# Storing the gate sigmoids beside the attention from GpSimd's queue, not ScalarE's

## The chip, the core and the metric

The kernel runs on one core of one Trainium2 chip. The core has five engines that matter here, each with its own instruction queue that is worked off in order: TensorE (PE in the profile, with PEld for its weight loads), VectorE (DVE), ScalarE (ACT), GpSimd (POOL) and SyncE (SP). ACT, POOL and SP can also issue DMA transfers; an issue stands in the queue of the engine that issues it. The metric is the device time of one execution in microseconds, lower is better, as the median of several runs.

## The reference

One layer of a streaming encoder trunk, in float32, for two request groups: 512 prompt tokens, and 8 streams of 16 tokens with cached keys and values. All 640 rows are worked together. Cut to what matters:

```python
parts = jnp.split(rms_norm(x, g_pre) @ w_in, points, axis=-1)
sb_q, sb_k, sb_v, sb_g, bd_q, bd_k, bd_v, bd_g, mm_q, mm_g, mg_sb, mg_bd, mg_mm = parts
o_sb = stick_breaking(...)      # 6 heads, strictly causal
o_bd = band_attention(...)      # 6 heads, softmax over a band, with a bias
o_mm = memory_attention(...)    # 4 heads into 256 memory tokens
merged = (jax.nn.sigmoid(mg_sb) * branch(o_sb, sb_g, w_up_sb)
          + jax.nn.sigmoid(mg_bd) * branch(o_bd, bd_g, w_up_band)
          + jax.nn.sigmoid(mg_mm) * branch(o_mm, mm_g, w_up_mem))
return x + rms_norm(merged @ w_out, g_post)
```

The three merge gates `mg_sb`, `mg_bd` and `mg_mm` are 2048 columns each, so 48 blocks of 128 columns. The change touches how the sigmoids of half of them reach memory.

## The kernel before, in words

Every float32 matrix product is made of three passes over operands that are split into a high and a low part (`split`, L118 to L120: ScalarE rounds the high part, VectorE subtracts it). Weights come by SP's queue into `wr` (L146) and are split into `wh` and `wl` (L119, L120), four buffers each.

The work runs in stages. First the memory projection and the normalisation of x. Then the projection of x, most of it in pairs of column blocks (`block_pair`, products at L760), up to about 1075 us of the profiled span. Next comes the attention, 16 heads in the order of `ORDER`, with the last 24 of the 48 gate blocks (`BESIDE`) spread among its steps as filler for TensorE. After it come the up-projections of the three branches, the merge and the output projection.

A gate block beside the attention is `gate_steps` (L694): 96 matmuls into a PSUM tile `acc` (L191, in four steps of 24), one ScalarE sigmoid from `acc` into `sig` (L698), and a store of `sig` to a DRAM tile `sig_d[i]` (L692) of 320 KB. `sig` has three buffers (pool `stg`). The same `put_sig` also stores the gates of the stage before (`put_gate`, L817). The stored gates are read back in the up-projections (L905), branch after branch, so the last 24 are read last.

`fill` (L920) pulls the next step of the filler; the attention's own matmuls stand between those steps, and `issue_after` chains the steps on TensorE in this order. The order of the other engines' queues, and the waits between them, are laid down when the kernel is compiled, from a simulated timeline (L1052).

A stick-breaking head takes, for each of four blocks of 128 queries: scores on TensorE into `s` (L176 to L178), two sigmoids on ScalarE into `b` and `e` (L430, L431), two masks on GpSimd (L433), a running product over `e` (L485) and a product with `b` (L487) on VectorE, and, about one filler step later on TensorE, the transposes of `b` into `tp` (L451). From `tp` ScalarE and VectorE make the split weights `wth` and `wtl`, and TensorE multiplies them with the values into `o`. The cached keys come in `kc` (L535, SP's queue), are transposed by VectorE into `kt` (L545) and multiplied at L549. GpSimd has little else in this stage: stores of new values (L643, L646) and of each head's result `osg_d` (L617), clears of `wth` and `wtl` (L445), and a mask product (L567).

Of the kernel before, what the change touches and what calls it, by code (L numbers as in the profile page):

```python
# [48 lines left out]
def stream_step_kernel(  # L49
# [8 lines left out]
    PE, ACT, DVE, POOL, SP = nc.tensor, nc.scalar, nc.vector, nc.gpsimd, nc.sync  # L58
# [42 lines left out]
    sig_d = [dpool.tile([P, NT], F32, name=f"sig_d{i}") for i in range(3 * KB)]  # L101
# [16 lines left out]
    def split(hi, lo, src):  # L118
        ACT.copy(hi, src)  # L119
        DVE.tensor_tensor(lo, src, hi.bitcast(F32), op=ALU.subtract)  # L120
# [79 lines left out]
    def x_proj_steps(col, acc):  # L200

        nonlocal last_mm, back
        steps, back = proj_steps(w_in, col, KB, x_src, acc, 8, back), False
        for _ in range(KB // 4):
            with tc.issue_after(last_mm or last_on(PE)):
                next(steps)
            last_mm = last_on(PE)
            yield
# [5 lines left out]
    def new_acc():  # L214
        return ps_acc.tile([P, 2, 512], F32, tag="acc", name="acc")

    def halves(t):
        return t.rearrange("p (s n) -> p s n", s=2)
# [469 lines left out]
    def operand(n, pool):  # L688
        return tuple(pool.tile([P, KH, HF], F32R, name=f"t{c}{n}") for c in "hl")

    def put_sig(i, sig):
        ACT.dma_start(sig_d[i], sig)  # L692

    def gate_steps(i):  # L694
        acc = new_acc()
        yield from x_proj_steps(C_GATE + i * P, acc)
        sig = stg.tile([P, NT], F32, tag="sig", name="sig")
        ACT.activation(halves(sig), acc[:, :, :HF], AF.Sigmoid)  # L698
        put_sig(i, sig)

    t2, t1 = operand(2, tpool), operand(1, tpool)
    tpool2 = gs.enter_context(tc.tile_pool(name="tpool2", bufs=1, reuse_waits="tile"))
# [23 lines left out]
    for i in range(FIRST):  # L726
        for _ in gate_steps(i):
            pass
        third.append(sums(2 * i))
# [80 lines left out]
    def put_gate(i):  # L810
        def put(n, t, q):
            if q is None:
                ACT.activation(t, t, AF.Sigmoid)
            else:
                ACT.activation(t[:, HF:], t[:, HF:], AF.Sigmoid)
                ACT.activation(t[:, :HF], q, AF.Sigmoid)
            put_sig(i + n, t)  # L817
        return put
# [46 lines left out]

    def fill_steps(done):
        for i in gates[-BESIDE:]:
            yield from gate_steps(i)

        xs.close()  # L870
        pm = br.enter_context(tc.tile_pool(name="mraw", bufs=1, side="right", reuse_waits="tile"))
        merged = pm.tile([P, KB, NT], F32, name="merged")
        po = br.enter_context(tc.tile_pool(name="osgp", bufs=6, side="right", reuse_waits="tile"))

        def load_o(i):
            r = po.tile([P, NT], F32, tag="sig", name="or", bufs=4)
            SP.dma_start(r, osg_d[i])
            hh = po.tile([P, NT], F32R, tag="oh", name="oh")
            ll = po.tile([P, NT], F32R, tag="ol", name="ol")
            split(hh, ll, r)  # L880
            return hh, ll

        for n, (w_up, nh, i0, g0) in enumerate(branches):
            while not done.issuperset(range(i0, i0 + nh)):
                yield
            parts = [load_o(i0 + h) for h in range(nh)]

            def o_src(k):
                return [[t[:, j * HF:(j + 1) * HF] for j in range(2)] for t in parts[k]]

            for j in range(KB):
                yield from up_steps(w_up, nh, o_src, j, n, merged[:, j], g0, po)
        up_done.append(merged)

    def up_steps(w_up, nh, src, j, n, m, g0, po):
        nonlocal last_mm
        acc = new_acc()
        steps = proj_steps(w_up[0], j * P, nh, src, acc)
        for _ in range((nh + 3) // 4):
            with tc.issue_after(last_mm):  # L900
                next(steps)
            last_mm = last_on(PE)
            yield
        sig = po.tile([P, NT], F32, tag="sig", name="sig", bufs=4)
        SP.dma_start(sig, sig_d[g0 + j])  # L905
        if n == 0:
            DVE.tensor_tensor(halves(m), acc[:, :, :HF], halves(sig), op=ALU.mult)
        else:
            DVE.tensor_tensor(halves(sig), acc[:, :, :HF], halves(sig), op=ALU.mult)
            POOL.tensor_tensor(m, m, sig, op=ALU.add)  # L910

    up_done = []
    with tc.tile_pool(name="att", bufs=1, reuse_waits="tile") as pa:
        qm, wTm = zero_padded(4)


        rest, done = iter(()), set()
        filler = fill_steps(done)

        def fill(n=1):  # L920
# [135 lines left out]
```

## Time and profile before

| what | us |
|---|---|
| median of 3 runs | 2049.0 |
| lowest and highest | 2047.3, 2050.6 |
| span of the profiled execution | 2044.4 |
| attention with the 24 gate blocks, in the span | about 1076 to 1545 |

Of the profiled execution the page gives the span alone, from its first to its last instruction. The clock that TensorE was granted has a mean of 0.997 over the span. In the views, a timeline row gives the start and the length in microseconds, the engine, the line of the kernel, the operation with output and input, and in square brackets how long the engine stood idle before it and what ended that. A row of waits gives the waiting engine and line, what it waited for, the total, the number and the longest. ACTq, SPq and POOLq are the instruction queues, where DMA issues stand.

### The profile page before, as it was taken

What the parts mean: (1) busy time and instruction counts of PE and PEld (TensorE: products, weight loads), DVE (VectorE), ACT (ScalarE), POOL (GpSimd) and SP (SyncE); (2) the same over time, 40 slices, a digit from 0 to 9 for tenths busy, and PEclk for the clock granted to TensorE, in tenths of its full rate; (3) what the DMA queues carried; (4) which work ended last, traced back from release to release, by engine and by line L of the source; (5) the groups of instructions that cost most, each with busy time, mean ns of one, the idle gap of its engine ahead of it and who ended that gap; (6) DMA issues with size and microseconds to landing.
All of it is one profiled execution on the core that took longest, in us unless ns stands there. A gap on an engine that the chain in (4) does not pass through costs nothing.

```text
span 2044.4 us, 35948 instructions
## 1 busy us (share of the span) xinstructions
PE 2014.2 (99%) x13829; PEld 1908.3 (93%) x13829; DVE 1178.5 (58%) x1830; ACT 839.1 (41%) x1577; POOL 705.8 (35%) x685
## 2 busy tenths in 40 slices
PE   8999999999999999999999999999999999999998
PEld 5999999999999999999998899999998899998886
DVE  6875577655676655555555555555556675442234
ACT  6544444444444444444443444444444332322221
POOL 1145566665666665644431011011010024330000
PEclk9999999999999999999999999999999999999999
DMA  7656676665686564663338777677679876532225
GB/s 269 218 140 150 169 207 142 168 168 149 161 205 154 137 156 130 150 150 111 118 106 280 224 221 219 214 225 225 211 214 283 255 234 178 144 123 83 73 93 216
DMA packets 548185, 361.38 MB, mean 177 GB/s; under 512 B 249169, under 2 KB 493409, under 8 KB 546477
## 3 DMA queue, kind: packets, MB, share of 16 engines
q1 hardware_dynamic: 528414, 305.80, 53.5%
q0 software_dynamic: 12688, 37.57, 5.5%
q10 hardware_dynamic: 6912, 15.73, 2.1%
q8 instruction: 108, 1.77, 0.4%
q14 instruction: 63, 0.52, 0.1%
HBM read 303.17 MB, written 90.77 MB: 193 GB/s over the span
## 4 chain that ended last, share of the span: by engine, by line
PE 91%; DMA 3%; DVE 2%; issue 1%; ACT 1%; POOL 1%; SPq 0%; ACTq 0%; DVEq 0%; POOLq 0%
PE q L760 44%; PE acc L191 27%; PE ya L176 4%; PE ya L178 4%; PE ya L177 4%; PE s L549 2%; PE o L608 1%; DMA or<-osg_d 1%; DVE wl L120 1%; PE tp L451 1%; PE acc L178 1%; PE acc L176 1%; PE acc L177 1%; PE o L177 1%; PE o L178 0%
## 5 line engine op out<-in xcount | busy, mean ns | idle before, releaser
L120 DVE TENSOR_TENSOR wl<-wr,wh 128x512 fp32r<-128x512 f32 (+1 forms) x516 | 411.7, 803 | 301.0 <-ACT wh L119 298.0
L119 ACT CAST wh<-wr 128x512 fp32r<-128x512 f32 (+1 forms) x516 | 311.7, 608 | 564.3 <-PE q L760 214.8
L120 DVE TENSOR_TENSOR wl<-ws,wh 128x512 fp32r<-128x512 f32 x304 | 285.1, 943 | 235.8 <-ACT wh L119 230.0
L760 PE MATMUL q<-xh,wl 128*128 128x320 f32 x1216 | 375.8, 309 | 0.3 <-DVE wl L120 0.3
L760 PE MATMUL q<-xh,wh 128*128 128x320 f32 x1216 | 375.7, 309 | 0.0
L760 PE MATMUL q<-xl,wh 128*128 128x320 f32 x1216 | 375.6, 309 | 0.0
L119 ACT CAST wh<-ws 128x512 fp32r<-128x512 f32 x304 | 188.1, 621 | 291.4 <-PE q L760 236.6
L760 PE MATMUL q<-th,wh 128*128 128x320 f32 x912 | 282.2, 309 | 2.0 <-ACT sig L777 2.0
L760 PE MATMUL q<-th,wl 128*128 128x320 f32 x912 | 281.9, 309 | 0.0
L760 PE MATMUL q<-tl,wh 128*128 128x320 f32 x912 | 281.8, 309 | 0.0
L760 PEld LDWEIGHTS q<-xh,wl 128*128 128x128 f32 x1216 | 228.7, 188 | 0.5 <-DVE wl L120 0.5
L760 PEld LDWEIGHTS q<-xl,wh 128*128 128x128 f32 x1216 | 228.6, 188 | 0.0
L760 PEld LDWEIGHTS q<-xh,wh 128*128 128x128 f32 x1216 | 228.5, 188 | 0.0
L191 PE MATMUL acc<-xh,wh 128*128 128x320 f32 x896 | 210.8, 313 | 0.0
L191 PE MATMUL acc<-xl,wh 128*128 128x320 f32 x896 | 209.5, 311 | 0.0
L191 PE MATMUL acc<-xh,wl 128*128 128x320 f32 x896 | 207.4, 310 | 0.0
L753 POOL TENSOR_TENSOR ws<-wr 128x512 f32<-128x512 f32 x114 | 169.1, 1496 | 81.2 <-DVE wl L120 68.5
L760 PEld LDWEIGHTS q<-th,wh 128*128 128x128 f32 x912 | 171.2, 188 | 2.7 <-ACT sig L777 2.5
L760 PEld LDWEIGHTS q<-th,wl 128*128 128x128 f32 x912 | 171.2, 188 | 0.2 <-DVE wl L120 0.2
L760 PEld LDWEIGHTS q<-tl,wh 128*128 128x128 f32 x912 | 171.2, 188 | 0.0
L191 PEld LDWEIGHTS acc<-xh,wh 128*128 128x128 f32 x896 | 150.1, 188 | 18.9 <-issue 18.4
L191 PEld LDWEIGHTS acc<-xl,wh 128*128 128x128 f32 x896 | 151.2, 188 | 0.6 <-issue 0.4
(228 smaller groups left out, 3353.1 us busy)
## 6 DMA issues: line engine op xcount, KB each, us to landing
wr<-in_w_in_dram SPq DMA_DIRECT2D x208, 512.0 KB, 4.9
kc<-keys_d SPq DMA_DIRECT2D x48, 512.0 KB, 5.8
wr<-in_w_out_dram SPq DMA_DIRECT2D x32, 512.0 KB, 3.7
sig_d<-sig ACTq DMA_DIRECT2D x48, 320.0 KB, 5.1
sig<-sig_d SPq DMA_DIRECT2D x48, 320.0 KB, 3.6
keys_d<-in_cache_sb_k_dram SPq DMA_DIRECT2D x96, 128.0 KB, 4.7
keys_d<-in_cache_band_k_dram SPq DMA_DIRECT2D x96, 128.0 KB, 4.5
vc<-in_cache_sb_v_dram SPq DMA_DIRECT2D x48, 256.0 KB, 5.6
```

Source lines behind the costliest of these rows:

```text
L119: ACT.copy(hi, src)
L120: DVE.tensor_tensor(lo, src, hi.bitcast(F32), op=ALU.subtract)
L176: PE.matmul(out, ah, bh, start=start, stop=False)
L177: PE.matmul(out, ah, bl, start=False, stop=False)
L178: PE.matmul(out, al, bh, start=False, stop=stop)
L191: PE.matmul(acc[:, s, :HF], a[:, k], b[s], start=first and f, stop=last and l)
L451: PE.transpose(tp[:, kb * P:(kb + 1) * P], b[:, kb * P:(kb + 1) * P], ident)
L549: return PE.matmul(s[32 * j:32 * j + 32, :nc_], qm[:, j, par * 32:par * 32 + 32], kts[j], start=par == 0, stop=par == 1, tile_position=(0, ...
L608: PE.matmul(o[32 * j:32 * j + 32, :P], l, r, start=i == 0, stop=i == len(steps) - 1, tile_position=(0, 32 * j))
L753: eng.tensor_tensor(o, a[c], b[c], op=op)
L760: PE.matmul(bank_, a[:, k], b[:, k], start=first and k == 0 and n == 0, stop=k == KH - 1 and n == 2, skip_group_check=not first)
```

## The change

`put_sig` and `gate_steps` take a queue, ScalarE's by default, and `fill_steps` passes GpSimd's. So the 24 stores of the gate blocks beside the attention are issued by POOL; the four gate blocks at the start and those of `put_gate` stay on ACT.

```diff
-    def put_sig(i, sig):
-        ACT.dma_start(sig_d[i], sig)
-
-    def gate_steps(i):
+    def put_sig(i, sig, queue=ACT):
+        queue.dma_start(sig_d[i], sig)
+
+    def gate_steps(i, queue=ACT):
...
-        put_sig(i, sig)
+        put_sig(i, sig, queue)
...
         for i in gates[-BESIDE:]:
-            yield from gate_steps(i)
+            yield from gate_steps(i, POOL)
```

## The prediction, made before the changed kernel was run

> **What bounds the kernel now.** I read the page's first part, then the busy times of the stretch 1076 to 1545 us, the only one the change touches.
>
> ```profile
> span 2044.4 us, 35948 instructions
> PE 2014.2 (99%) x13829; PEld 1908.3 (93%) x13829; DVE 1178.5 (58%) x1830; ACT 839.1 (41%) x1577; POOL 705.8 (35%) x685
> ...
> 1076.00:1545.00 469.00, 462.24 (x3733) 428.39 (x3731) 258.99 (x529) 209.44 (x416) 47.38 (x130) 0.99 0.74 229
> ```
>
> The columns of the last row are PE, PEld, DVE, ACT and POOL. PE is busy for 462.2 of 469.0 us, ACT for 45% and POOL for 10%. Relieving ACT or loading POOL therefore counts only where PE waits for one of them. So the second view is PE's waits in that stretch, which are all of these:
>
> ```profile
> PE tp L451 <- DVE b L487: 4.3, 1, 4.3
> PE o L176 <- ACT wth L119: 2.3, 1, 2.3
> PE tp L451 <- DVE b L497: 0.2, 1, 0.2
> ```
>
> One wait of 4.3 us is most of it. The third view is ACT's timeline before it, the fourth the chain of waits through it.
>
> ```profile
> 1090.26 0.70 ACT L698 ACTIVATE sig<-acc 128x640 f32<-128x640 f32 x1
> 1101.03 0.39 ACTq L692 DMA_DIRECT2D sig_d<-sig  x1
> 1101.47 0.58 ACT L119 CAST wth<-tp 128x512 fp32r<-128x512 f32 x1 [10.51 <-DMA kc<-keys_d]
> ```
> ```profile
> 1093.66 7.30 DMA kc<-keys_d
> ...
> 1100.98 0.02 ACTq L692
> ...
> 1102.45 0.39 ACT e L431
> ...
> 1102.90 0.30 POOL e L433
> ...
> 1104.68 0.56 DVE b L487
> ...
> 1105.38 0.88 PE tp L451 x3
> ...
> 1106.89 3.88 PE acc L191 x21
> ...
> 1110.89 0.44 PE acc L191 x3
> 1111.33 0.12 PE s L176
> ```
>
> The first gate's sigmoid ends at 1090.96, but its store is issued only at 1101.03, 10.07 us later, right when a load of cached keys, issued by SP, lands. `sig` and `kc` share no data, so I take it that the store waits on a completion count that the two transfers share. ACT's queue is in order: behind the store stand the cast of `wth`, then the sigmoids L430 and L431, and from them the chain runs over POOL's mask, DVE's product and PE's transposes. I conclude this from the ACTq step in the chain: the cast itself needs `tp`, which PE had made by about 1094.4 (below), and no `kc`.
>
> The Trainium skill, "DMA: Bandwidth & Descriptors", section "Why a DMA increments its semaphore by 16 and not by 1", says that two transfers in flight on one semaphore can be mistaken for each other and asks for one semaphore per slot in flight. A store that waits for the earlier holder of its semaphore is what that would lead to; the trace shows the wait, not the semaphore's number.
>
> **What the change removes.** The store leaves ACT's queue, so the cast could run when `tp` is ready.
>
> ```profile
> 1093.81 0.60 PE L451 MATMUL tp<-ident,b 128*128 128x128 f32 x4
> ...
> 1094.77 0.31 PE L191 MATMUL acc<-xh,wh 128*128 128x320 f32 x1
> ...
> 1100.79 0.31 PE L191 MATMUL acc<-xh,wh 128*128 128x320 f32 x1
> ```
>
> The scores s are done by about 1095, so what took 4.28 us from L430's start at 1101.95 to the transposes at 1105.38 (3.4 us) would end near 1098.5, before PE gets there at 1100.94 (1100.79 plus a matmul's pace). The stall of 1105.38 − 1100.94 = **4.44 us** goes.
>
> ```profile
> 687.53 387.68 PE q L760 x2640
> ...
> 1106.00:1110.00 4.00, 4.00 (x22) 4.00 (x21) 3.96 (x8) 1.76 (x4) 0.96 (x3) 0.69 1.11 343
> ```
>
> The pace undisturbed is 387.68 / 2640 = 0.147 us a matmul. After the stall the granted clock is 0.69 in 1106 to 1110 us. From 1105.38 to 1111.33 PE took 5.95 us for 3 transposes, 3 scores, 24 gate matmuls and one L176. At full clock that is at most 0.96 us for the transposes and scores (the four and three of 1093.81 to 1094.77), 24 × 0.147 = 3.53, and 0.12: 4.61. So another **1.34 us** goes. If the clock dips all the same, this term is nothing.
>
> What is late next at that place? The second pair of keys, and the weights of the next gate steps:
>
> ```profile
> 1096.10 1.43 SPq L535 DMA_DIRECT2D kc<-keys_d  x1
> ...
> 1098.66 2.16 SPq L146 DMA_DIRECT2D wr<-in_w_in_dram  x1
> ...
> DMA to landing us min/median/max: 7.3/7.5/7.8
> ...
> 1102.70 1.15 ACT L119 CAST wh<-wr 128x512 fp32r<-128x512 f32 x2
> ...
> 1111.61 1.05 PE L549 MATMUL s<-kt,qm 128*32 128x512 f32 x4
> ```
>
> The keys land by 1096.10 + 7.8 = 1103.9, and the matmuls on them would come at 1111.6 − 5.8 = 1105.8; two transposes of DVE lie between (the row at L545 below: 0.65 us each). The weight casts ran at 1102.70 back to back, so their data was there by then; one is used at once, the other a step later. I take nothing for this; at worst 1 us comes back.
>
> ```profile
> 1105.15 1.30 DVE L545 STREAM_TRANSPOSE kt<-kc 128x512 f32<-128x512 f32 x2
> L692 ACTq DMA_DIRECT2D sig_d<-sig x25: 326/327/393, 1076.1 to 1540.5; - x25
> L837 POOL DMA_DIRECT2D raw_d<-sig x28: 540/558/591, 158.4 to 780.4; - x28
> ```
>
> The other 23 stores free ACT for 23 × 0.327 = 7.5 us in all, of which PE gets nothing: it waits for ACT only once more (2.3 us). That wait is set by a table load and the last sigmoid, not by a store:
>
> ```profile
> 1538.46 1.28 ACT L698 ACT_TABLE_LOAD   x1
> 1539.75 0.70 ACT L698 ACTIVATE sig<-acc 128x640 f32<-128x640 f32 x1
> ```
>
> **What it adds.** 24 stores on POOL, of the size of the 28 at L837: 24 × 0.558 = 13.4 us, which raises POOL from 47.4 to 60.8 us of 469, or 13%. POOL's work in this stage that PE hangs on is the pair of masks. Each store needs the sigmoid done on ACT, a wait that is new on POOL; behind it queue the next masks, clears or head stores. In the order of time the closest POOL instruction behind a sigmoid's end is this one:
>
> ```profile
> 1331.71 0.70 ACT L698 ACTIVATE sig<-acc 128x640 f32<-128x640 f32 x1
> ...
> 1333.29 0.54 POOL L617 DMA_DIRECT2D osg_d<-sg  x1 [0.98 <-DVE sg L616]
> ```
>
> 0.88 us lie between, more than 0.558. So, if POOL's queue keeps the order of time, no mask is delayed: nothing. The upper bound is in the rivals. A store may itself stand behind POOL's waits, of which the longest in the stretch is 23.7 us:
>
> ```profile
> POOL wtl L445 <- PE o L177: 147.9, 15, 23.7
> ```
>
> That delays only the release of `sig`, which has three buffers for a gate every (1539.75 − 1090.26) / 23 = 19.5 us, and the reads come later, the 24 last gates at the end. Nothing again. The `put_gate` stores, and everything ahead of 1076 us, stay.
>
> A rule of the Trainium skill speaks against the change. "SBUF — State Buffer", section "SBUF: two separate sides", says that a DMA issued from GpSimd has its descriptors written by GpSimd's cores, which a VectorE instruction that holds the shared port pair locks out, and "A bandwidth-pool intuition that's wrong (but worth ruling out)" gives 3100 ns for a DMA that takes 620 alone; by it the sum would get up to 24 × 2.5 = 60 us of POOL time, an estimate from that page. The L837 rows disagree: 28 stores, beside a VectorE that is busy 63% of that stage, all took 0.540 to 0.591 us.
>
> ```profile
> 150.00:850.00 700.00, 698.49 (x4760) 697.77 (x4759) 444.18 (x507) 293.55 (x527) 453.56 (x385) 1.00 0.64 159
> ```
>
> **The sum.** 4.44 + 1.34 = 5.8 us, bounds 3.4 (the clock dip stays, 1 us comes back) and 8.1 (the wait of 2.3 us goes too). The profiled execution's span would be 2038.6. The span lies 4.6 us under the median of the runs, which I take as what lies around it: 2049.0 − 5.8 = **2043.2 us**. A measurement can tell about 0.2% here, 4.1 us.
>
> **The rivals.** (1) *The wait moves along with the store.* If the store on POOL also waits for the keys, the mask behind it (1102.90 in the chain) is as late as now and the same stall stands: 2049. Against it: the stores at L837 wait for SP's loads hardly at all.
>
> ```profile
> POOL raw_d L837 <- DMA keys_d<-in_cache_band_k_dram: 0.9, 3, 0.3
> ```
>
> (2) *The orders are laid down anew.* The queues follow a simulated timeline (L1052), and a store off ACT changes it. One more stall of the 2.3 us kind with its clock dip costs about 3.6 us, so a single one leaves 2046.8, and two make 2050.4: within 0.2%. Against it: the stalls are very few, since almost everything has a filler step of slack.
>
> (3) *Slower: POOL stands ahead of its masks.* If a store stands before a mask whose input is ready, the mask waits for the sigmoid. Its price: table load, sigmoid, store.
>
> ```profile
> L698 ACT ACT_TABLE_LOAD  x12: 1283/1283/1283, 1140.9 to 1538.5; - x12
> ```
>
> 1.28 + 0.70 + 0.56 = 2.54 us each where PE has no slack, in up to 12 gates (those with a table load). From the third one the gain is gone (5.8 / 2.54 = 2.3), from the fourth it is slower by over 0.2%; six give 2049.0 − 5.8 + 15.2 = 2058.4, all twelve 2073.7. For it: the transposes can follow the masks closely, 2.5 us at 1102.90 to 1105.38. Against it: the order of time above, and a step of 24 × 0.147 = 3.5 us of filler before most transposes.
>
> (4) *VectorE holds the stores up.* If a store can't be written while a VectorE instruction runs, it waits for the end of it, at most about as long as this one:
>
> ```profile
> 1103.22 0.96 DVE L485 TENSOR_TENSOR_SCAN e<-e 128x384 f32<-128x384 f32 x1 [0.44 <-POOL e L433]
> ```
>
> If all 24 did, and PE felt each, that is 23 us on the sum, 2066; the L837 rows leave it hardly a chance. This is the mechanism of the Trainium skill's rule above ("SBUF — State Buffer").
>
> That the change doesn't do what it says isn't possible: `fill_steps` passes POOL to all 24.
>
> **Chances.** Forecast as it stands, 2041.5 to 2044.9: 0.50. More than that, if the other small waits go too: 0.05. Rival 1: 0.08. Rival 2 and a part-gain within 0.2%: 0.20. Rival 3, with a bad new order among its causes: 0.16. Rival 4: 0.01. So faster 0.55, same 0.28, slower 0.17. The range runs from 2040.5 to 2055: about 0.03 lies under it and 0.11 above.
>
> **What would show it.** Right: in the changed trace no ACT idle of 10 us near 1091, L692 on POOL with about 0.56 us each, no PE wait at L451 near 1101, the granted clock back at 1.00 there, the attention ending near 1539 instead of 1545, and the same distance from there to the end. Wrong: a POOL wait on `kc` or on `sig` of several us with a PE wait on L451 behind it; or PE waits at new places; or the 5.8 us given back at the change to the up-projections, where PE now waits for `or`.

## The result, and the profile after

The changed kernel takes 2045.3 us (median of 20 runs, 2040.5 to 2047.9) against 2048.95 for the kernel before (20 runs, 2044.1 to 2054.5). The ratio is 0.998 with a 95% interval of 0.9973 to 0.9987, so 2.7 to 5.5 us less, 4.1 by the ratio. The forecast was 5.8 us less.

The first part of the page of the changed kernel, and PE's waits in its attention stage:

```profile
span 2044.8 us, 36000 instructions
PE 2016.7 (99%) x13829; PEld 1910.4 (93%) x13829; DVE 1178.1 (58%) x1830; ACT 837.9 (41%) x1577; POOL 719.3 (35%) x709
```

```profile
PE o L176 <- ACT wth L119: 2.3, 1, 2.3
PE acc L191 <- DVE ol L120: 0.6, 1, 0.6
PE s L549 <- DVE kt L545: 0.5, 1, 0.5
```

The wait of 4.3 us at L451 is gone, the one of 2.3 us stands as before, and two short ones are new. Yet this span is no shorter than the 2044.4 us of before: single executions of one kernel differ by several microseconds, as the medians' ranges show, so two spans alone decide nothing here. Note also that PE is busy 2.5 us longer (2014.2 before) with the same 13829 matmuls. Two things that lengthen it are found below.

ACT's timeline of the changed kernel at the place of the old stall, and POOL's:

```profile
1091.92 0.70 ACT L698 ACTIVATE sig<-acc 128x640 f32<-128x640 f32 x1
1096.10 0.59 ACT L119 CAST wth<-tp 128x512 fp32r<-128x512 f32 x1 [3.48 <-PE tp L451]
...
1110.18 0.62 ACT L119 CAST wh<-wr 128x512 fp32r<-128x512 f32 x1 [6.00 <-DMA wr<-in_w_in_dram]
```

```profile
1093.96 0.54 POOL L692 DMA_DIRECT2D sig_d<-sig  x1
1097.19 0.29 POOL L433 TENSOR_SCALAR_AFFINE_SELECT b<-b 128x128 f32<-128x128 f32 x1 [2.69 <-ACT b L430]
```

The cast of `wth` now waits 3.48 us for `tp`, which it needs, where it stood idle for 10.51 us until the keys `kc` had landed, which it does not need. POOL issues the store at 1093.96, and the mask behind it waits for ACT's sigmoid, not for the store.

To compare executions that start at different moments I use the 24 sigmoids of the beside gates as marks. From the last projection matmul to the first of them it is the same in all of them, so the distance from the first to the last is the time of the stage. Here are the 1st, 2nd, 8th, 16th and 24th in ACT's timeline of the changed kernel, then the 2nd, the 8th and the 16th of the kernel before (its 1st, 1090.26, and 24th, 1539.75, stand in the prediction):

```profile
1091.92 0.70 ACT L698 ACTIVATE sig<-acc 128x640 f32<-128x640 f32 x1
...
1114.90 0.70 ACT L698 ACTIVATE sig<-acc 128x640 f32<-128x640 f32 x1
...
1231.27 0.71 ACT L698 ACTIVATE sig<-acc 128x640 f32<-128x640 f32 x1
...
1384.20 0.71 ACT L698 ACTIVATE sig<-acc 128x640 f32<-128x640 f32 x1
...
1536.92 0.70 ACT L698 ACTIVATE sig<-acc 128x640 f32<-128x640 f32 x1
```

```profile
1118.57 0.70 ACT L698 ACTIVATE sig<-acc 128x640 f32<-128x640 f32 x1
...
1236.29 0.70 ACT L698 ACTIVATE sig<-acc 128x640 f32<-128x640 f32 x1
...
1388.13 0.70 ACT L698 ACTIVATE sig<-acc 128x640 f32<-128x640 f32 x1
```

| stretch between sigmoids | before | changed | difference |
|---|---|---|---|
| 1st to 8th (head) | 146.03 | 139.35 | −6.68 |
| of these, 1st to 2nd | 28.31 | 22.98 | −5.33 |
| of these, 2nd to 8th | 117.72 | 116.37 | −1.35 |
| 8th to 16th (a repeat) | 151.84 | 152.93 | +1.09 |
| 16th to 24th (a repeat) | 151.62 | 152.72 | +1.10 |
| 1st to 24th | 449.49 | 445.00 | −4.49 |

So the stretch with the stall, from the 1st to the 2nd mark, gives 5.33 us. The rest of the head gives another 1.35 us that the stall can't account for, and 2.2 us are **given back** in the two repeats, where neither kernel has a stall to speak of. That is what the experiments had to explain.

### The profile page after: what moved, and what is told of

It is laid out like the page before. It is cut to its first block, busy times and chain, and to the rows that moved or that the text cites. A ratio compares the mean times of both kernels' runs of the same rounds, so it can differ in the third digit from the quotient of the medians.

```text
span 2044.8 us, 36000 instructions
## 1 busy us (share of the span) xinstructions
PE 2016.7 (99%) x13829; PEld 1910.4 (93%) x13829; DVE 1178.1 (58%) x1830; ACT 837.9 (41%) x1577; POOL 719.3 (35%) x709
## 4 chain that ended last, share of the span: by engine, by line
PE 93%; DMA 2%; DVE 1%; issue 1%; ACT 1%; POOL 1%; SPq 0%; DVEq 0%; ACTq 0%; POOLq 0%
PE q L760 45%; PE acc L191 29%; PE ya L178 4%; PE ya L176 4%; PE ya L177 4%; PE s L549 2%; PE o L608 1%; PE tp L451 1%; POOL merged L910 1%; PE o L177 1%; PE o L178 0%; PE o L176 0%; DMA kc<-keys_d 0%; PE s L176 0%; PE s L177 0%
## 5 line engine op out<-in xcount | busy, mean ns | idle before, releaser
L800 POOL TENSOR_TENSOR ws<-wr,ws 128x512 f32<-128x512 f32 x76 | 100.0, 1316 | 148.4 <-DVE wl L120 147.7
```

The lines of the kernel that those rows point to most:

```text
L800: POOL.tensor_tensor(b, a, b, op=ALU.subtract)
```

## The experiments

**Theory**: the gain is the first of the 24 stores alone, which waited on ACT's queue for a load with which it shares a completion count; what is given back comes from the new order of TensorE's queue. **Rivals**: the 23 other stores bring the gain (ACT relieved) or the loss (POOL loaded); or the wait belongs to any store at that moment, not to ACT's queue.

All runs were made beside runs of the kernel before, and the ratio is to those, so ratios compare better between rows than medians. "Order" is TensorE's compiled order: A that of the kernel before, B that of the changed kernel, C a third one (below). "Stage" is the time from the 1st to the 24th beside sigmoid in the profiled execution.

| run | stores of the beside gates | order | median us | ratio, 95% interval | stall at L451 | stage |
|---|---|---|---|---|---|---|
| before | 24 ACT | A | 2048.95 | | 4.3 | 449.5 |
| before_again | 24 ACT | A | 2047.5 | 0.9995, 0.9983 to 1.0007 | 3.6 | 449.6 |
| e_rest | first ACT, 23 POOL | B | 2049.3 | 1.0005, 0.9995 to 1.0016 | 2.7 | 448.7 |
| e_tiny | 24 POOL, and 64 bytes on ACT | B | 2050.7 | 1.0012, 1.0004 to 1.0021 | 3.6 | 448.2 |
| the change | 24 POOL | B | 2045.3 | 0.998, 0.9973 to 0.9987 | none | 445.0 |
| after_again | 24 POOL | B | 2045.3 | 0.9982, 0.9973 to 0.999 | none | 444.4 |
| after_third | 24 POOL | B | 2044.3 | 0.998, 0.9971 to 0.9989 | none | 445.7 |
| e_split | 15 POOL, 9 ACT | B | 2042.9 | 0.9977, 0.9968 to 0.9985 | none | 444.5 |
| e_first | first POOL, 23 ACT | A | 2043.8 | 0.9975, 0.9966 to 0.9984 | none | 444.4 |
| e_first_sp | first SP, 23 ACT | A | 2044.0 | 0.9976, 0.9965 to 0.9987 | none | 443.9 |
| e_whole | 21 POOL, 3 ACT | C | 2039.8 | 0.9969, 0.9957 to 0.9981 | none | 441.4 |
| e_whole_again | 21 POOL, 3 ACT | C | 2041.1 | 0.9967, 0.9955 to 0.998 | none | 441.9 |
| e_whole_sp | 24 SP | C | 2041.6 | 0.9973, 0.9962 to 0.9984 | none | 441.1 |

### e_first and e_rest: the first store alone, and all but the first

```diff
-            yield from gate_steps(i, POOL)
+            yield from gate_steps(i, POOL if i == gates[-BESIDE] else ACT)
```

> Only the first of the 24 gate blocks beside the attention stores from GpSimd's queue; the other 23 store from ScalarE's, and TensorE, VectorE and SyncE keep the order of before. Theory 1 (the one store that waits for the keys is what costs): the whole gain and no new order, so 5.8 to 6.7 us under before, near 2043, and one to two us under the changed kernel; no TensorE wait at L451 near 1101. Rival (ScalarE gains by being rid of 24 issues): a 24th of the gain, 0.2 us, no difference from before.

e_first: 2043.8 us, ratio 0.9975. ACT's timeline has the cast waiting for `tp`, as in the changed kernel, and the marks are these:

```profile
1088.69 0.70 ACT L698 ACTIVATE sig<-acc 128x640 f32<-128x640 f32 x1
1093.54 0.59 ACT L119 CAST wth<-tp 128x512 fp32r<-128x512 f32 x1 [4.15 <-PE tp L451]
...
1229.64 0.71 ACT L698 ACTIVATE sig<-acc 128x640 f32<-128x640 f32 x1
...
1381.47 0.70 ACT L698 ACTIVATE sig<-acc 128x640 f32<-128x640 f32 x1
...
1533.08 0.70 ACT L698 ACTIVATE sig<-acc 128x640 f32<-128x640 f32 x1
```

One store moved makes the head 140.95 us, 5.1 less than before, and leaves the repeats at 151.83 and 151.61. The other half:

```diff
-            yield from gate_steps(i, POOL)
+            yield from gate_steps(i, ACT if i == gates[-BESIDE] else POOL)
```

> The first gate block stores from ScalarE's queue as before, the other 23 from GpSimd's; TensorE's order is that of the changed kernel. Theory 1: the store still waits for the keys, ScalarE idle for about 10 us and TensorE for about 4.4 near 1101; and the new order of TensorE costs about 1 us in each of two repeats, so 0 to 2 us over before (2049 to 2051). Rival: 23 of 24 parts of the gain, 3.5 us under before.

e_rest: 2049.3 us, ratio 1.0005. Its waits of PE and its ACT timeline have the old picture again:

```profile
PE tp L451 <- DVE b L487: 2.7, 1, 2.7
```

```profile
1097.68 0.59 ACT L119 CAST wth<-tp 128x512 fp32r<-128x512 f32 x1 [8.91 <-DMA kc<-keys_d]
```

So the whole gain is the first store's, and relieving ACT of 23 others brings nothing.

### e_tiny: what the store waited for

To the changed kernel is added one transfer of 64 bytes on ACT's queue, at the place of the first store, into a DRAM tile that nothing reads.

```diff
-        put_sig(i, sig, queue)
+        put_sig(i, sig, queue); i == 40 and ACT.dma_start(tiny_d, sig[0:1, 0:16])
```

> The changed kernel, with one transfer of 64 bytes added that ScalarE issues behind the first gate's sigmoid, in the place where the store stood. Theory 1 (what costs is an issue in ScalarE's queue that has to wait for a completion count it shares with the keys, not what it moves): the 10 us of ScalarE's idle time and the stall of 4.4 us are back, 0 to 2 us over before. Rival (the store's 320 KB, or its share of the transfers, is what costs): as the changed kernel, about 3.7 us under before.

e_tiny: 2050.7 us, ratio 1.0012. (The median lies 2 us over that of before, which its stage, 448.2 us, doesn't show; this stays open.) The stall is back, with 64 bytes in place of 320 KB. Its ACT timeline, then PE's wait:

```profile
1091.86 0.70 ACT L698 ACTIVATE sig<-acc 128x640 f32<-128x640 f32 x1
1101.83 0.48 ACTq L699 DMA_DIRECT2D tiny_d<-sig  x1
1102.35 0.59 ACT L119 CAST wth<-tp 128x512 fp32r<-128x512 f32 x1 [9.79 <-DMA kc<-keys_d]
```

```profile
PE tp L451 <- DVE b L487: 3.6, 1, 3.6
```

The size and the data play no part, then. The traces also hold the number of the semaphore (the completion count) that each DMA issue counts on and waits for, which the views leave out. It names the cause: in these traces the issues of ACT and SP share eight numbers (100 to 102 and 105 to 109), those of POOL use eight of their own (111 to 118), and ACT's store is given number 105, on which the load of the keys is still in flight. It is issued only when that load has landed.

| run | issue at the place of the first store | issued at | waits for | counts on |
|---|---|---|---|---|
| before | ACT, L692 `sig_d` | 1101.03 | 105, last used by SP's load of `kc` at 1093.66, and the sigmoid | 105 |
| e_rest | ACT, L692 `sig_d` | 1097.32 | 105, last used by SP's load of `kc` at 1090.48, and the sigmoid | 105 |
| e_tiny | ACT, L699 `tiny_d` | 1101.83 | 105, last used by SP's load of `kc` at 1094.26, and the sigmoid | 105 |
| the change | POOL, L692 `sig_d` | 1093.96 | the sigmoid | 117 |

The page "DMA: Bandwidth & Descriptors" of the Trainium skill, section "Why a DMA increments its semaphore by 16 and not by 1", asks for one semaphore per slot in flight. Here, where two queues share eight, an unrelated load in flight cost ACT's queue 10.07 us (before).

### before_again: how constant is the stall?

The kernel before, unchanged.

> The kernel before, unchanged, for a second trace and for the clock of each of its runs. If the dip of TensorE's clock near 1733 us, which the changed kernel's trace has and the first trace of before has not, comes by chance in both kernels, the runs fall into two groups some 3 us apart, the slower with a mean clock lower by 0.002 to 0.003. If the change brings it, the runs of before form one group. Time: no difference.

Ratio 0.9995, as it should be. The dip near 1733 us, which the expectation asks about, is in this trace too: over 1722 to 1745 us the granted clock is 0.93, where it is 1.00 in the first trace of before. So the change doesn't bring it. The twelve runs part as the expectation says for chance: five took 2043.6 to 2045.1 us at mean clocks of 0.995 to 0.997, seven 2047.1 to 2052.3 us at 0.993 to 0.994.

The stall is 3.6 us here. With 4.3 (before), 2.7 (e_rest) and 3.6 (e_tiny) the four executions that have it show 3.6 us in the mean, and the one from which I forecast was the longest. The clock behind it is not constant either. Around the stall it is 0.94 in before, in before_again and in e_rest, but 1.00 in e_tiny, whose stall was no shorter than that of before_again. The rows of before and of e_tiny (the last columns are clock, DMA share and GB/s):

```profile
1085.00:1112.00 27.00, 22.72 (x145) 20.94 (x145) 14.60 (x23) 7.98 (x17) 3.04 (x8) 0.94 1.07 327
```

```profile
1085.00:1112.00 27.00, 23.38 (x158) 21.11 (x156) 15.16 (x25) 8.89 (x21) 3.88 (x10) 1.00 1.08 332
```

### e_first_sp: is it POOL, or anything but ACT?

```diff
-            yield from gate_steps(i, POOL)
+            yield from gate_steps(i, SP if i == gates[-BESIDE] else ACT)
```

> Only the first gate's store is moved, to SyncE's queue, in place of GpSimd's; all other orders are those of before. There it stands behind a load issued at about 1101, when the keys have landed, so it should hold nothing up. If what counts is only that the store is off ScalarE's queue: as with the first store on GpSimd's, about 5 us under before, and from the last matmul of the projections to the eighth gate's sigmoid 156 us (161.4 before). If GpSimd's queue itself is what helps, or if SyncE's loads are held up behind the store: less, down to no gain and 161 us.

2044.0 us, ratio 0.9976, the same as from POOL. The store still counts on semaphore 105, so it is the place in ACT's queue that made the shared count dear. SP issues the store late, 14.5 us after the start of the sigmoid at 1093.56, and it does not matter: no wait of PE comes of it, and `sig` has three buffers. SP's timeline and the sigmoids' row (first and last start at its end):

```profile
1108.07 0.42 SPq L692 DMA_DIRECT2D sig_d<-sig  x1
```

```profile
L698 ACT ACTIVATE sig<-acc x24: 696/704/727, 1093.6 to 1537.5; 128x640 f32<-128x640 f32 x24
```

### after_again, after_third: the changed kernel once more

> The changed kernel again, beside the run above on the same chip: 3.7 to 4.1 us under before. In the trace the two repeats of 152.9 us and 152.7 us between the gates' sigmoids (151.8 and 151.6 with the order of before) should stand to 0.1 us, since the order fixes them, and the dip of the clock near 1733 should be there or not, by chance, and move the end by about 3 us.

> The changed kernel, unchanged, as the measure for the run beside it: median 2045, ratio to before 0.998; from the first beside sigmoid to the last 445 us.

Ratios 0.9982 and 0.998, stages of 444.4 and 445.7 us: the result stands. In both traces the repeats take 152.93 and 152.72 us, and the 2nd to the 8th mark 116.37 us, as in the first. What differs between executions of this kernel is the stretch from the 1st to the 2nd mark (22.98, 22.40 and 23.65 us).

### e_whole, e_whole_sp, e_split: what is given back

In the repeats PE waits nowhere, so I compared its timelines matmul by matmul. The memory heads' score matmuls (L549, operands 128*32) differ. The kernel before, then the changed one, each with the row that follows the group:

```profile
1378.01 0.64 PE L549 MATMUL s<-kt,qm 128*32 128x256 f32 x8
1378.57 0.56 PE L191 MATMUL acc<-xh,wh 128*128 128x320 f32 x2
```

```profile
1373.32 0.62 PE L549 MATMUL s<-kt,qm 128*32 128x256 f32 x2
1373.87 0.44 PE L506 MATMUL tp<-ident,b 128*128 128x128 f32 x2
...
1374.60 0.63 PE L549 MATMUL s<-kt,qm 128*32 128x256 f32 x6
1375.16 0.56 PE L191 MATMUL acc<-xh,wh 128*128 128x320 f32 x2
```

Eight together hold PE for 0.56 us (1378.01 to 1378.57). Split, the two take 0.55 and the six 0.56: each group costs the same, however many are in it, so the split costs 0.55 us. A repeat has two such groups, and both are split: 1.1 us, the difference found above. No wait row shows it, since PE counts as busy.

The eight records (x8) are four matmuls (`score`, L549), each for another 32-column part of TensorE's array (the expectation below calls them row-tiled, but it is the columns), and the times say that the four run side by side: one of them alone holds PE as long as all four. The page "TensorEngine Tiling (Array Packing)" of the Trainium skill, section "Key Properties", says that changing the tiling mode drains TensorE. The trace puts most of the price elsewhere, since a fixed charge for the change of form would not grow with the matmul: the groups with 512 columns in place of 256 take 0.98 to 0.99 us, as a split in the head shows. It stands in order A (the kernel before) and not in order B (last row, the changed kernel, whose next matmul starts at 1128.41):

```profile
1129.84 1.04 PE L549 MATMUL s<-kt,qm 128*32 128x512 f32 x2
1130.82 0.66 PE L589 MATMUL tp<-ident,b 128*128 128x128 f32 x4
...
1132.20 1.06 PE L549 MATMUL s<-kt,qm 128*32 128x512 f32 x6
1133.19 0.56 PE L191 MATMUL acc<-xh,wh 128*128 128x320 f32 x2
```

```profile
1127.42 1.06 PE L549 MATMUL s<-kt,qm 128*32 128x512 f32 x8
```

So the new order mends one split in the head, worth 0.98 us, while it makes the others. Together with the wait of 0.2 us at L451 behind L497, which only order A has, that is 1.2 of the 1.35 us that the 2nd to the 8th mark gained.

But the kernels with the split are also those with the most stores on POOL. To part the two, I looked for an assignment of queues whose compiled order has no split although most stores are on POOL. With only the 5th, 13th and 21st store on ACT there is one (order C, whole in all three repeats; A is split in the first, B in all):

```diff
-        for i in gates[-BESIDE:]:
-            yield from gate_steps(i, POOL)
+        for n, i in enumerate(gates[-BESIDE:]):
+            yield from gate_steps(i, ACT if n in (4, 12, 20) else POOL)
```

> All of the beside stores on POOL but three (the 5th, 13th and 21st gate, on ACT). In the compiled order of TensorE, the row-tiled score matmuls L549 of the memory heads (32x256) then stand together in all eight gate repeats, where the changed kernel splits them, twice in each of three repeats. Theory 'the split costs the time': from the 8th to the 16th and to the 24th sigmoid it takes 151.8 and 151.6 us as before, not 152.9 and 152.7; with the first repeat unsplit too, 2.2 to 3.3 us less than the changed kernel, a median of 2042 to 2043. Rival 'the stores on POOL cost the time, whatever the order': 21 of 24 are still there, so 21/24 of the 2.2 us stays: 152.8 and 152.6 us, median about 2045.

With the same order C, all 24 stores on SP:

```diff
-            yield from gate_steps(i, ACT if n in (4, 12, 20) else POOL)
+            yield from gate_steps(i, SP)
```

> All 24 beside stores on SP. The compiled orders of TensorE and VectorE are those of the kernel with three stores on ACT and the rest on POOL, with no split. Theory 'the order alone sets it, the queue only matters through it': both repeats within 0.1 us of that kernel's, median within 1 us of it. Rival 'the queue of the stores counts for itself': on SP they hold up loads of weights and keys behind a sigmoid; new PE waits at L191 or L549, 1 us or more in all, and a median of 2045 or above.

And with order B, the stores next to the split groups on ACT:

```diff
-            yield from gate_steps(i, ACT if n in (4, 12, 20) else POOL)
+            yield from gate_steps(i, ACT if n % 8 > 4 else POOL)
```

> Stores of the 6th to 8th gate of each eight on ACT (9 in all), of the others on POOL (15). The compiled orders of TensorE, VectorE and SP are those of the changed kernel, with the split. The split groups lie beside the 7th and 8th gate of each eight, whose stores are now on ACT. Theory 'the split costs the time': repeats of 152.9 and 152.7 us as in the changed kernel, median 2044.5 to 2046. Rival 'the stores on POOL cost it': 15 of 24 are left, so repeats of about 152.5 and 152.3, median about 2044.5 or less.

The marks of e_whole (1st, 8th, 16th, 24th), of e_whole_sp and of e_split (8th, 16th, 24th):

```profile
1088.78 0.70 ACT L698 ACTIVATE sig<-acc 128x640 f32<-128x640 f32 x1
...
1226.65 0.70 ACT L698 ACTIVATE sig<-acc 128x640 f32<-128x640 f32 x1
...
1378.50 0.70 ACT L698 ACTIVATE sig<-acc 128x640 f32<-128x640 f32 x1
...
1530.13 0.70 ACT L698 ACTIVATE sig<-acc 128x640 f32<-128x640 f32 x1
```

```profile
1229.48 0.70 ACT L698 ACTIVATE sig<-acc 128x640 f32<-128x640 f32 x1
...
1381.33 0.70 ACT L698 ACTIVATE sig<-acc 128x640 f32<-128x640 f32 x1
...
1532.96 0.70 ACT L698 ACTIVATE sig<-acc 128x640 f32<-128x640 f32 x1
```

```profile
1230.46 0.70 ACT L698 ACTIVATE sig<-acc 128x640 f32<-128x640 f32 x1
...
1383.40 0.70 ACT L698 ACTIVATE sig<-acc 128x640 f32<-128x640 f32 x1
...
1536.12 0.70 ACT L698 ACTIVATE sig<-acc 128x640 f32<-128x640 f32 x1
```

| repeat | e_whole, 21 on POOL | e_whole_sp, 24 on SP | e_split, 15 on POOL |
|---|---|---|---|
| 8th to 16th | 151.85 | 151.85 | 152.94 |
| 16th to 24th | 151.63 | 151.63 | 152.72 |

This is as clean as such things get: with 21 stores on POOL the repeats take what they took with none, and with nine stores back on ACT they take what the changed kernel takes. The order sets the time; the stores on POOL cost TensorE nothing, and those on SP nothing either. e_split's median (2042.9) came lower than I expected, and by itself it would fit the rival as well. Its repeats and its stage of 444.5 us are those of the changed kernel, and its ratio, 0.9977, lies within the changed kernel's intervals.

In e_whole the head is 137.87 us (1226.65 − 1088.78), 1.5 less than in the changed kernel. From the 2nd to the 8th mark it takes 115.26 us, 1.1 less, since its first repeat is whole too; the rest is in the first stretch, which varies. Its median of 2039.8 us lay below the 2042 to 2043 expected, so I ran it once more beside the changed kernel.

> The kernel with 21 beside stores on POOL and the 5th, 13th and 21st on ACT once more, beside the changed kernel on the same chip. By the split theory it is 3.3 us (three repeats by 1.1) below the changed kernel, give or take what the medians leave open: 2040 to 2042.5, ratio to before 0.9965. If its first median of 2039.8 was six lucky runs, it comes out within 1 us of the changed kernel.

2041.1 us against 2044.3 (after_third) on the same chip: 3.2 us less, where three repeats by 1.1 make 3.3. It beats both kernels: 0.9967 to before here and 0.9969 the first time. The intervals overlap a little with those of the changed kernel, so that the step from the one to the other rests on both repetitions and on the stage, 441.9 us here.

## Why the prediction was right, step by step

- **The bound and its cause: right.** One wait of PE, made by one store on ACT's queue that waits for the keys' completion count. e_first and e_rest place the whole gain in that store, e_tiny shows that neither its size nor its data matter, and the traces give both transfers the same semaphore, which the prediction could only take to be so.
- **4.44 + 1.34 = 5.8 us for the stall and the clock behind it: right in kind, a little long.** By e_first the stage is 5.1 us shorter than that of before (449.49 to 444.39), by e_first_sp 5.6, by the ratio of e_first 5.1 (0.0025 × 2048.7). The stall of the execution I read was the longest of four, and the clock dip that I priced at 1.34 us followed it in three of the four, not in e_tiny. So the price varies: the stages of e_rest and e_tiny are only 3.7 and 3.2 us longer than that of the changed kernel, whose order they share. One figure of that working is wrong: from L430's start at 1101.95 to the transposes at 1105.38 it is 3.43 us, not 4.28. The 3.4 in brackets is right, and the 1098.5 follows from it.
- **The other 23 stores worth nothing to PE: right** (e_rest, 1.0005).
- **24 × 0.558 = 13.4 us on POOL, hidden: right.** POOL is busy 719.3 − 705.8 = 13.5 us longer, in this stage PE has no wait that comes from POOL, and e_whole's repeats show no cost.
- **What is late next, up to 1 us: right in the main.** The second keys make PE wait 0.5 us at L549 in the changed kernel's trace, not at all in after_again, and 1.2 us in after_third, a little over the bound. The wait of 6.00 us for `wr` at 1110.18 ends in no wait of PE.
- **Rival 1, the wait moves along: no.** POOL's store went at 1093.96, 1.34 us after the sigmoid's end at 1092.62, where ACT's came 10.07 us after its own.
- **Rival 2, the orders laid anew: it came true in part, beside the forecast, and by another mechanism.** I looked for new stalls of some 3.6 us each and argued that they are few. What came is no stall: matmuls that stood together are split, at 0.55 us a group, 2.2 us in the two repeats. The head gained 1.35 us in return (2nd to 8th mark, 117.72 us in order A with and without the stall, 116.37 in order B), of which 1.2 are the mended split and the short wait behind it; the last 0.15 us are open. Net, +0.85 us.
- **Rival 3, POOL ahead of its masks, and rival 4, VectorE holding up POOL's stores: no.** The row of the 24 stores on POOL in the changed kernel (minimum, median and maximum in ns):

```profile
L692 POOL DMA_DIRECT2D sig_d<-sig x24: 542/543/560, 1094.0 to 1537.9; - x24
```

 None took longer than 0.56 us beside VectorE; the rule that the prediction took from the Trainium skill, "SBUF — State Buffer", section "SBUF: two separate sides", does not show here.

- **The step that was off: the mapping from the span to the median.** I took the 4.6 us between span and median for what lies around the span. The changed kernel's profiled run took 2046.5 us with a span of 2044.8, so only 1.7 lie around it; the profiled execution of before was a quick one, by about 2.9 us. The sum survives that since it is a difference. A sign that the prediction named did not show in the changed kernel's first trace: from the last mark to the end it took 507.88 us, not the 504.66 of before. The clock dip shown in the last section accounts for it; in after_again, which has no such dip, it took 504.64. What the sum should have been: 5.1 to 5.6 for the stall, less 0.85 for the order, so 4.2 to 4.8, against 4.1 measured (2.7 to 5.5).
- **The size, in the prediction's own bands: a little less than forecast.** The median of 2045.3 us lies just above the 2041.5 to 2044.9 that had a chance of 0.50, where the prediction put rival 2 and a part-gain (0.20). The direction, the wait and the store were foreseen; that the new order would take part of the gain in busy time was not.

## What to carry to other kernels

A DMA issue on a compute engine's queue can wait for a transfer it has nothing to do with; when an engine stands idle until data land that its next instruction doesn't use, look at the issue ahead of that instruction and move that one issue, not the whole class. A queue change also changes the compiled order everywhere else: compare the time of like stretches, not only the waits, since the price can lie in busy time. Where matmuls that use different parts of TensorE's array stand together, keep them together: one alone holds the array as long as four did here.

## What the runs showed of the hardware that I had not expected

- A group of 128*32 matmuls costs TensorE 0.55 to 0.56 us with two, six or eight records in it at 256 columns, and 0.98 to 0.99 us at 512. So the price is mostly the time of one matmul, and the others of the group run beside it. By a line through both widths, an estimate, some 0.12 us are left that do not depend on the width; whether that is the change of form wasn't tried.
- The granted clock can fall beside waits far shorter than the stall above, and does so in one execution and not in another. In the changed kernel it fell at the start of the band branch, beside waits of 0.53, 1.16 and 0.75 us, in the profiled execution:

```profile
1729.81 0.56 PE L191 MATMUL acc<-oh,wh 128*128 128x320 f32 x2 [0.53 <-ACT oh L119]
1731.54 0.56 PE L191 MATMUL acc<-ol,wh 128*128 128x320 f32 x2 [1.16 <-DVE ol L120]
...
1733.14 0.90 PE L191 MATMUL acc<-oh,wh 128*128 128x320 f32 x2 [0.75 <-ACT oh L119]
```

 Over 1722 to 1745 us its clock was 0.85 in the mean (first row), so 23 × 0.15 = 3.4 us of full clock were missing. In another execution of the same kernel (after_again, second row) the clock was whole there, with waits of 0.72, 1.01 and 0.30 us:

```profile
1722.00:1745.00 23.00, 20.56 (x116) 19.41 (x115) 12.65 (x17) 7.82 (x13) 6.04 (x5) 0.85 0.63 195
```

```profile
1722.00:1745.00 23.00, 20.93 (x137) 19.82 (x136) 12.83 (x18) 8.63 (x15) 7.22 (x5) 1.00 0.62 192
```

 That is part of why PE's busy time and the span of the changed kernel's profile did not fall, and of the spread of some 7 us between the runs of one kernel. A saving of 4 us shows in medians of many runs and in the marks, not in two spans.
